# Low halves of weight pieces: which come by an accumulating DMA, which by subtraction, and how far ahead they are split

## The chip, the core and the metric

The kernel runs on one NeuronCore of a Trainium2 chip. The metric is the device time of one execution, in microseconds (us). The core has a TensorE (PE in the profile; PEld is its weight load), a VectorE (DVE), a ScalarE (ACT), a GpSimd (POOL), and a SyncE (SP) that issues DMAs. Each engine works through its own instructions in order and waits for others by semaphores. DMAs run beside them on 16 DMA engines.

## The reference

Two blocks of two layers each, batch 1, 512 tokens, width 1024, all in float32. Cut to its structure:

```
for l in range(2):                          # first block
    proj = rms_norm(h, g_mix) @ w_in        # q, k, v, recurrence and gate
    h += concat(diff_attention, rg_lru * gelu) @ w_out
    h += square(relu(rms_norm(h, g_mlp) @ w_mlp_in)) @ w_mlp_out
    h += sigmoid(rms_norm(h, g_ple) @ w_ple_gate) * (p @ w_ple_proj)     # "PLE"
x = rms_norm(h, g_final)
for l in range(2):                          # second block
    proj = rms_norm(x, g_pre_mix) @ w_in_2  # pool, q, k, v and an indexer
    x += rms_norm(concat(pool_mixer, topk_attention) @ w_out_2, g_post_mix)
    x += rms_norm(square(relu(rms_norm(x, g_pre_ffn) @ w_ff1_2)) @ w_ff2_2, g_post_ffn)
```

## The kernel before

**Pieces.** The weights are cut into pieces of 128 partitions x 1024 float32 (512 KB; the indexer's pieces have 512 or 656 columns), listed in `PLAN` (L102) in the order in which TensorE uses them. A piece has two k-blocks. It is split into two float32r halves: `wh`, the value rounded by ScalarE (L201), and `wl`, what is left. A product is three matmuls: high by high, high by low and low by high, so a piece of 512 columns is 24 matmuls, eight times a group of three.

**How a piece gets there.** `w_load` (L181) loads it by SP's queue into one of two `raw` buffers. `w_conv` (L188) makes `wh` on ScalarE and then `wl` in one of two ways. For the weights named in `ON_POOL` (L103: `w_in`, `index`, `w_in_2`, `w_out`, `w_out_2`) and the first four pieces of `w_ff1_2`, ScalarE writes the negated high half into `wl` (L206) and GpSimd issues a DMA that adds the weights from HBM onto it (L209). For all others VectorE subtracts (L211). The very first piece is always subtracted on VectorE.

**How far ahead.** `take` (L223) hands a piece to the matmuls and calls `w_ahead` (L214) first. That loads and splits pieces up to `LC` (L32) positions further on in `PLAN`, up to `LH` for kept ones, and loads one more (`LD` less `LC`). `wh` and `wl` have three buffers each (L159), one more than `LC`: a new piece needs the buffers of the piece that ended last.

**Kept pieces.** `gemm_h` (L254) goes through its pieces twice, for two halves of the tokens. Some of them are put in `keep` and get buffers of their own (tag `F`, in a pool that is opened after the attention's pool `mx` has closed). `keep_in` (L295) is called when a stage opens (L383 to L385, L576); the indexer's kept pieces of the second layer are listed at L1439. A piece that was split before its name came into `keep` sits in the ordinary buffers.

**Order.** A planner with a cost model puts the instructions of each engine in order, by the order in which the program writes them and by priorities; `urgent` raises one, and `behind` (L111) pins one instruction behind another on its engine. `bcast` (L412) broadcasts a row of scales through TensorE; splits are pinned behind the last one. `rsqrt` (L380) runs on GpSimd and notes itself in `st["rsqrt"]`.

**Sums of squares.** `Stat.add` (L389) squares on ScalarE and adds to `acc` on the engine named by `eng`; `Stat.mean` (L398) sums over partitions with small matmuls (B<-ones,acc), after which `rsqrt` gives the norm's scale. In PLE (`ev_g`, L986) the sums `st4` and, in the second layer, `st5` are added on GpSimd.

The stages in order of time: first block layer 0 (to 652 us), layer 1 (to 1264), indexer and attention of the second block layer 0 (1264 to 1485), its feed-forward (to 1879), then the same for layer 1. In the second block the feed-forward begins with `w_out_2` and `w_ff1_2` by `gemm_h` (L393, L571).

Of the kernel before, what the change touches and what calls it, by code (L numbers as in the profile page):

```python
# [8 lines left out]
F32 = mybir.dt.float32  # L9
F32R = mybir.dt.float32r  # L10
I32 = mybir.dt.int32
# [14 lines left out]
PC = 1024  # L26
ORDER = {"w_out": (4, 5, 6, 7, 0, 1, 2, 3), "w_out_2": (2, 3, 0, 1, 4, 5, 6, 7)}
NX = 11

URGENT = 250  # L30

LD, LC, LH = 3, 2, 3  # L32
IDX_SCALE = 8 ** -0.5
ALL = slice(0, 512)
HALVES = (slice(0, 256), slice(256, 512))
# [66 lines left out]
PLAN = _plan()  # L102
ON_POOL = ("w_in", "index", "w_in_2", "w_out", "w_out_2")  # L103
# [3 lines left out]
def two_blocks_kernel(ctx: ExitStack, tc: tile.TileContext, io):  # L107
    nc = tc.nc
    V, A, G, SY = nc.vector, nc.scalar, nc.gpsimd, nc.sync

    def behind(r, last):  # L111

        tc.add_manual_dep(r.ins, last.name, mybir.DependencyInfo(
            mybir.DependencyClass.NoSync, mybir.DependencyReason.DATA), reason="issue order")
# [24 lines left out]
    xp = ctx.enter_context(tc.tile_pool(name="acts", bufs=1))  # L139
# [8 lines left out]
    class Tags:  # L148
# [5 lines left out]
        def __call__(self, tag, dt=None, shape=None):  # L154
# [1 line left out]
            return self.pool.tile(shape or sh, dt or d, name=nm(tag), tag=tag, bufs=n)  # L156

    C512 = [128, 512]
    P = Tags(xp, X=([128, 2, 512], F32R, NX), raw=([128, PC], F32, 2), wh=([128, PC], F32R, 3),  # L159
             wl=([128, PC], F32R, 3), sn=([128, 8], F32, 4), v4=([128, 4], F32, 4), ri=([128, 4], I32, 2),  # L160
             rh=([128, 4], F32, 2), rt=([128, 4], F32, 2), rs=([128, 4], F32, 3), acc=(C512, F32, 2),
             mn=([128, 1], F32, 6), sm=([128, 4], F32, 6), sq=([128, 8], F32, 3), iw=([128, 8], F32, 4),
             m8=([128, 8], F32, 6))
# [6 lines left out]
    st = {"i": 0, "ld": 0, "cv": 0}  # L170
    raws, his, los, keep = {}, {}, {}, {}
# [9 lines left out]
    def w_load():  # L181
        i = st["ld"]
        st["ld"] += 1
        n = PLAN[i][4] * PLAN[i][5]
        raws[i] = P("raw")
        SY.dma_start(raws[i][:, :n], where[i])

    def w_conv():  # L188
        i = st["cv"]
        st["cv"] += 1  # L190
        n = PLAN[i][4] * PLAN[i][5]
        r = raws.pop(i)
        h_, l_ = keep[PLAN[i]]() if PLAN[i] in keep else (P("wh"), P("wl"))
        if i == 0:
            for a in range(0, n, n // 2):
                b = slice(a, a + n // 2)
                A.activation(h_[:, b], r[:, b], AF.Copy)  # L197
                V.tensor_sub(l_[:, b], r[:, b], h_[:, b].bitcast(F32))
            his[i], los[i] = h_, l_
            return  # L200
        g = A.activation(h_[:, :n], r[:, :n], AF.Copy)  # L201
        if "bcast" in st:
            behind(g, st["bcast"].ins)
        if PLAN[i][0] in ON_POOL or PLAN[i][0] == "w_ff1_2" and PLAN[i][2] == 0:

            g = A.activation(l_[:, :n], r[:, :n], AF.Copy, scale=-1.0)  # L206
            if "bcast" in st:
                behind(g, st["bcast"].ins)
            G.dma_start(l_[:, :n], where[i], accum_op=OP.add)  # L209
        else:  # L210
            V.tensor_sub(l_[:, :n], r[:, :n], h_[:, :n].bitcast(F32))  # L211
        his[i], los[i] = h_, l_
# [131 lines left out]
    h = [const.tile([128, S], F32, name=f"h{k}") for k in range(8)]  # L344
# [77 lines left out]
    X = [None] * 8  # L422
# [498 lines left out]
    def block1(l, X, fac, last):  # L921
        C = mix1(l, X, fac)
        X2, X3, X4 = [None] * 8, [None] * 8, [None] * 8
        with tc.tile_pool(name=nm("pp"), bufs=1) as ppool:
# [7 lines left out]
            with tc.tile_pool(name=nm("ff"), bufs=1) as fp:  # L932
# [10 lines left out]
                for g in range(2):  # L943
                    run(gemm_t(C[0:4], "w_out", l, g * 512, 4, 4, [bank() for _ in range(4)],
                               lambda c, p_, g=g: ev_o(g * 4 + c, p_)))
# [20 lines left out]
            with tc.tile_pool(name=nm("pl"), bufs=1) as lp:  # L966
                L = Tags(lp, prj=(C512, F32, 8), t=(C512, F32, 3),
                         q=(C512, F32, 2), sb=(C512, F32, 1))
                s3b = L("sb")

                s3 = P("v4")

                @urgent
                def mk_s3():
                    rsqrt(s3, st3.mean())

                st4, st5 = Stat(lambda: L("q")), Stat(lambda: L("q")) if last else None
                for g in range(2):
                    prj = []

                    def ev_p(c, p_):
                        t_ = L("prj")
                        A.activation(t_, p_, AF.Copy, scale=0.5)
                        prj.append(t_)

                    def ev_g(c, p_, g=g):  # L986
                        k = g * 4 + c
                        t_ = L("t")
                        V.tensor_mul(t_, p_, s3b)
                        A.activation(t_, t_, AF.Tanh, scale=0.5)  # L990
                        V.scalar_tensor_tensor(t_, t_, 1.0, prj[c], op0=OP.add, op1=OP.mult)
                        V.tensor_add(h[k], h[k], t_)
                        X4[k] = P("X")
                        split(X4[k], h[k], gff[:, k:k + 1] if last else col("g_mix", l + 1, k))
                        st4.add(h[k], eng=G)
                        if last:
                            st5.add(h[k], scale=col("g_final", 0, k), eng=G)

                    run(gemm_t(Pt, "w_ple_proj", l, g * 512, 0, 2, [bank() for _ in range(4)], ev_p))
                    run(gemm_t(X3, "w_ple_gate", l, g * 512, 0, 8, [bank() for _ in range(4)], ev_g),  # L1000
                        at={1: mk_s3, 4: lambda: bcast(s3, s3b)} if g == 0 else None)
# [25 lines left out]
    for l in range(DEPTH):  # L1027
        X, fac = block1(l, X, fac, l == DEPTH - 1)
# [468 lines left out]
    for l in range(DEPTH):  # L1497
        X, fac, ahead = block2(l, X, fac, ahead, l == DEPTH - 1)
# [74 lines left out]
```

## Time and profile before

| | us |
|---|---|
| median of 3 runs (2511.75 to 2515.87) | 2513.86 |
| the profiled execution's own time | 2513.39 |
| its span, first to last instruction | 2511.6 |
| TensorE busy | 2395.1 (95%) |
| VectorE busy | 1290.8 (51%) |
| ScalarE busy | 1197.6 (48%) |
| GpSimd busy | 297.2 (12%) |

The time outside the span is 1.8 us. "Busy" counts instructions that run; a waiting engine is idle, and the profile names what ended the wait. A line's number is that of the kernel before; most instructions of VectorE and TensorE go through a helper at L126, so they are told apart by their tiles.

### The profile page before, as it was taken

The numbers are of one execution on the slowest core, as the hardware profiler recorded it, in microseconds if no ns is written. First come the engines' busy times: TensorE is split into PE (matmuls) and PEld (weight loads), VectorE is DVE, ScalarE is ACT, GpSimd is POOL, SyncE is SP. The second block draws the span as 40 slices with busy tenths as digits, with TensorE's granted clock in tenths as the row PEclk, the third lists the DMA queues.
The fourth block names the chain that finished last, engine by engine and source line by source line (L and its number), as shares of the span: only waits on it lengthen the run. The fifth ranks groups of instructions, "written<-read, shape, count | busy, mean of one in ns | idle before, by whom it ended". The sixth has DMA issues, their size and how long they took to land.

```text
span 2511.6 us, 30853 instructions
## 1 busy us (share of the span) xinstructions
PE 2395.1 (95%) x11700; PEld 1993.6 (79%) x11700; DVE 1290.8 (51%) x2524; ACT 1197.6 (48%) x2051; POOL 297.2 (12%) x509
## 2 busy tenths in 40 slices
PE   7999999999999999999989989999998998999997
PEld 5778888888777888888778778888897777888887
DVE  4586433435458643343549847323345974632434
ACT  5785322324578532242456875323336587432321
POOL 1310000000231000000143212000012311100000
PEclk8999999999999999999989999999999999999999
DMA  7744233332774432333267452323345736232232
GB/s 191 166 103 125 93 94 99 93 96 89 167 168 101 111 99 93 101 93 94 79 144 157 113 129 73 101 93 93 101 107 125 168 83 136 68 101 92 93 101 68
DMA packets 80647, 276.19 MB, mean 110 GB/s; under 512 B 9073, under 2 KB 11505, under 8 KB 80497
## 3 DMA queue, kind: packets, MB, share of 16 engines
q1 hardware_dynamic: 62208, 211.22, 27.0%
q0 software_dynamic: 18288, 62.99, 14.6%
q8 instruction: 92, 1.51, 0.2%
q14 instruction: 59, 0.48, 0.1%
HBM read 272.08 MB, written 2.10 MB: 109 GB/s over the span
## 4 chain that ended last, share of the span: by engine, by line
PE 77%; DVE 9%; ACT 8%; DMA 3%; issue 2%; POOL 1%; SPq 0%; DVEq 0%; POOLq 0%; ACTq 0%
PE B L126 77%; ACT xe L643 1%; DVE ac L126 1%; DMA wl<-in_w 1%; DMA F<-in_w 1%; DVE fo L126 1%; DVE m L126 1%; DVE xe L126 1%; ACT wh L201 1%; DVE rn L126 1%; DVE X L126 1%; POOL acc L396 1%; DVE h L126 1%; ACT xe L1259 1%; ACT wl L206 1%
## 5 line engine op out<-in xcount | busy, mean ns | idle before, releaser
L126 PE MATMUL B<-X,wh 128*128 128x512 f32 (+1 forms) x3072 | 952.4, 392 | 7.0 <-ACT wh L197 7.0
L201 ACT ACTIVATE wh<-raw 128x1024 fp32r<-128x1024 f32 (+2 forms) x370 | 386.5, 1046 | 837.3 <-PE B L126 810.8
L126 DVE TENSOR_TENSOR wl<-raw,wh 128x1024 fp32r<-128x1024 f32 (+1 forms) x262 | 321.8, 1229 | 740.3 <-ACT wh L201 738.9
L126 PEld LDWEIGHTS B<-X,wh 128*128 128x128 f32 x3072 | 561.7, 189 | 111.5 <-ACT wh L197 7.0
L126 PE MATMUL B<-X,wl 128*128 128x512 f32 (+1 forms) x1536 | 596.3, 388 | 17.5 <-DMA wl<-in_w 16.0
L126 PE MATMUL B<-F,wh 128*128 128x512 f32 (+1 forms) x2048 | 608.6, 381 | 0.0
L126 PEld LDWEIGHTS B<-F,wh 128*128 128x128 f32 x2048 | 375.8, 188 | 81.9
L126 PE MATMUL B<-F,wl 128*128 128x512 f32 (+1 forms) x1024 | 389.9, 381 | 0.0
L126 PEld LDWEIGHTS B<-X,wl 128*128 128x128 f32 x1536 | 290.4, 189 | 78.9 <-DMA wl<-in_w 16.9
L126 PE MATMUL B<-wh,X 128*128 128x512 f32 (+2 forms) x960 | 293.7, 382 | 1.3 <-DMA wh<-in_wx 0.8
L126 PEld LDWEIGHTS B<-F,wl 128*128 128x128 f32 x1024 | 192.3, 188 | 40.9
L126 PEld LDWEIGHTS B<-wh,X 128*128 128x128 f32 x960 | 177.5, 192 | 33.2 <-issue 1.9
L126 PE MATMUL B<-wl,X 128*128 128x512 f32 (+2 forms) x504 | 181.6, 375 | 11.3 <-DMA wl<-in_wx 7.1
L206 ACT ACTIVATE wl<-raw 128x1024 fp32r<-128x1024 f32 (+2 forms) x110 | 111.8, 1016 | 62.6 <-PE B L126 62.4
L209 POOL DMA_DIRECT2D wl<-in_w x99 | 87.0, 882 | 441.7 <-ACT wl L206 344.5
L126 DVE TENSOR_TENSOR f<-r 128x512 f32<-128x512 f32 (+1 forms) x136 | 89.8, 664 | 61.3 <-ACT r L562 61.2
L562 ACT ACTIVATE r<-B 128x512 f32<-128x512 f32 (+1 forms) x136 | 76.4, 566 | 86.4 <-PE B L126 83.6
L126 PEld LDWEIGHTS B<-wl,X 128*128 128x128 f32 x504 | 95.2, 196 | 28.2 <-DMA wl<-in_wx 7.6
L126 PE MATMUL B<-X,F 128*128 128x256 f32 x576 | 80.4, 298 | 26.3 <-DMA F<-in_w 15.9
L126 PEld LDWEIGHTS B<-X,F 128*128 128x128 f32 x576 | 75.2, 201 | 30.1 <-DMA F<-in_w 16.3
L381 POOL TENSOR_TENSOR v<-v,nhalf 128x4 f32<-128x4 f32 (+1 forms) x8 | 8.6, 1070 | 764.1 <-DVE v L126 764.1
L126 DVE TENSOR_TENSOR F<-f,F 128x512 fp32r<-128x512 f32 (+1 forms) x136 | 88.5, 654 | 1.3 <-ACT F L370 1.0
(214 smaller groups left out, 2495.3 us busy)
## 6 DMA issues: line engine op xcount, KB each, us to landing
raw<-in_w SPq DMA_DIRECT2D x380, 512.0 KB, 3.5
wl<-in_w POOLq DMA_DIRECT2D x99, 512.0 KB, 7.9
F<-in_w POOLq DMA_DIRECT2D x12, 512.0 KB, 8.3
raw<-in_wx SPq DMA_DIRECT2D x8, 328.0 KB, 3.2
h<-in_xT SPq DMA_DIRECT2D x8, 256.0 KB, 7.1
raw<-in_wx SPq DMA_DIRECT2D x8, 256.0 KB, 2.7
out<-h SPq DMA_DIRECT2D x16, 128.0 KB, 1.8
wl<-in_wx POOLq DMA_DIRECT2D x5, 328.0 KB, 5.3
```

The lines of the kernel that those rows point to most:

```text
L126: r = f(*a, **k)
L201: g = A.activation(h_[:, :n], r[:, :n], AF.Copy)
L206: g = A.activation(l_[:, :n], r[:, :n], AF.Copy, scale=-1.0)
L209: G.dma_start(l_[:, :n], where[i], accum_op=OP.add)
L381: st["rsqrt"] = G.tensor_tensor(y, v, nhalf[:, :y.shape[-1]], op=OP.pow)
L396: eng.tensor_add(self.acc[:, ts], self.acc[:, ts], q_[:, ts])
L562: A.activation(r_[:, :n], p_, AF.Relu)
L643: A.activation(e[:, :n], e[:, :n], AF.Exp, scale=-1.0, bias=mn, accum_out=sums)
L1259: A.activation(e[:, :n], e[:, :n], AF.Copy, scale=sm[:, 1:2])
```

## The change

It raises `LD`, `LC` and `LH` from 3, 2, 3 to 4, 3, 4 and gives `wh` and `wl` a fourth buffer. The reserve for DMA descriptors is set to 8192 bytes per partition, half of what it is when not named. In `w_conv` the accumulating DMA stays for pieces of `ON_POOL` that are not the indexer's, not kept, and not among the first four of the plan. The other pieces that had it are subtracted: on VectorE those of the indexer's first layer, on GpSimd the rest (pieces 1 to 3 of `w_in`, the indexer's second layer, the kept ones), in two halves of the columns, pinned behind the last `rsqrt` that the program has written by then. The sum `st4` in PLE goes to VectorE.

By the code, of 127 accumulating DMAs 98 are left: 3 first pieces, 16 of the indexer, 2 of `w_out_2` and 8 of `w_ff1_2` no longer have one. Of the two kept pieces of `w_out_2` per layer the earlier one is now split before `keep_in` is called, so it sits in the ordinary buffers and keeps its DMA.

```diff
@@ -29,7 +29,7 @@
 
 URGENT = 250
 
-LD, LC, LH = 3, 2, 3
+LD, LC, LH = 4, 3, 4
 IDX_SCALE = 8 ** -0.5
 ALL = slice(0, 512)
 HALVES = (slice(0, 256), slice(256, 512))
@@ -156,8 +156,8 @@
             return self.pool.tile(shape or sh, dt or d, name=nm(tag), tag=tag, bufs=n)
 
     C512 = [128, 512]
-    P = Tags(xp, X=([128, 2, 512], F32R, NX), raw=([128, PC], F32, 2), wh=([128, PC], F32R, 3),
-             wl=([128, PC], F32R, 3), sn=([128, 8], F32, 4), v4=([128, 4], F32, 4), ri=([128, 4], I32, 2),
+    P = Tags(xp, X=([128, 2, 512], F32R, NX), raw=([128, PC], F32, 2), wh=([128, PC], F32R, 4),
+             wl=([128, PC], F32R, 4), sn=([128, 8], F32, 4), v4=([128, 4], F32, 4), ri=([128, 4], I32, 2),
              rh=([128, 4], F32, 2), rt=([128, 4], F32, 2), rs=([128, 4], F32, 3), acc=(C512, F32, 2),
              mn=([128, 1], F32, 6), sm=([128, 4], F32, 6), sq=([128, 8], F32, 3), iw=([128, 8], F32, 4),
              m8=([128, 8], F32, 6))
@@ -201,12 +201,18 @@
         g = A.activation(h_[:, :n], r[:, :n], AF.Copy)
         if "bcast" in st:
             behind(g, st["bcast"].ins)
-        if PLAN[i][0] in ON_POOL or PLAN[i][0] == "w_ff1_2" and PLAN[i][2] == 0:
+        if PLAN[i][0] in ON_POOL and PLAN[i][0] != "index" and PLAN[i] not in keep and i > 3:
 
             g = A.activation(l_[:, :n], r[:, :n], AF.Copy, scale=-1.0)
             if "bcast" in st:
                 behind(g, st["bcast"].ins)
             G.dma_start(l_[:, :n], where[i], accum_op=OP.add)
+        elif PLAN[i][0] in ON_POOL and PLAN[i][:2] != ("index", 0) or PLAN[i][0] == "w_ff1_2" and PLAN[i][2] == 0:
+            for a in range(0, n, n // 2):
+                b = slice(a, a + n // 2)
+                g = G.tensor_sub(l_[:, b], r[:, b], h_[:, b].bitcast(F32))
+                if "rsqrt" in st:
+                    behind(g, st["rsqrt"].ins)
         else:
             V.tensor_sub(l_[:, :n], r[:, :n], h_[:, :n].bitcast(F32))
         his[i], los[i] = h_, l_
@@ -992,7 +998,7 @@
                         V.tensor_add(h[k], h[k], t_)
                         X4[k] = P("X")
                         split(X4[k], h[k], gff[:, k:k + 1] if last else col("g_mix", l + 1, k))
-                        st4.add(h[k], eng=G)
+                        st4.add(h[k])
                         if last:
                             st5.add(h[k], scale=col("g_final", 0, k), eng=G)
 
@@ -1560,7 +1566,7 @@
     from concourse.bass_utils import run_bass_kernel_spmd as _run
 
     arrays = layout(inputs)
-    nc = _bacc.Bacc("TRN2", target_bir_lowering=False, num_devices=1)
+    nc = _bacc.Bacc("TRN2", target_bir_lowering=False, num_devices=1, dynamic_dma_scratch_size=8192)
     io = {}
     for name, a in arrays.items():
         io[name] = nc.dram_tensor(f"in_{name}", a.shape, mybir.dt.from_np(a.dtype), kind="ExternalInput").ap()
```

## Rows read from the trace of the kernel before

**Rows 1.** The page: span, busy times, landing times of DMAs (last number, us)
```profile
span 2511.6 us, 30853 instructions
...
PE 2395.1 (95%) x11700; PEld 1993.6 (79%) x11700; DVE 1290.8 (51%) x2524; ACT 1197.6 (48%) x2051; POOL 297.2 (12%) x509
...
raw<-in_w SPq DMA_DIRECT2D x380, 512.0 KB, 3.5
wl<-in_w POOLq DMA_DIRECT2D x99, 512.0 KB, 7.9
```

**Rows 2.** What TensorE waited for: us in total, times, longest
```profile
PE B L126 <- DMA wl<-in_w: 20.2, 3, 11.3
PE B L126 <- DMA F<-in_w: 15.9, 2, 8.0
...
PE B L126 <- DMA wl<-in_wx: 7.1, 2, 5.6
...
PE B L126 <- DMA F<-in_wx: 4.2, 2, 3.4
```

**Rows 3.** TensorE's timeline at its waits: start us, length, [idle before <- releaser]
```profile
26.61 0.80 PE L126 MATMUL B<-X,wl 128*128 128x512 f32 x1 [11.34 <-DMA wl<-in_w]
...
661.77 0.80 PE L126 MATMUL B<-X,wl 128*128 128x512 f32 x1 [4.67 <-DMA wl<-in_w]
...
1282.04 0.64 PE L126 MATMUL B<-wl,X 128*128 128x328 f32 x1 [5.56 <-DMA wl<-in_wx]
...
1308.01 0.50 PE L126 MATMUL B<-wl,X 128*128 128x512 f32 x1 [4.15 <-DMA wl<-in_w]
...
1493.34 7.01 PE L126 MATMUL B<-X,F 128*128 128x256 f32 x46 [7.87 <-DMA F<-in_w]
...
1896.49 3.37 PE L126 MATMUL B<-F,X 128*128 128x328 f32 x11 [3.40 <-DMA F<-in_wx]
...
2108.95 7.99 PE L126 MATMUL B<-X,F 128*128 128x256 f32 x46 [8.01 <-DMA F<-in_w]
```

**Rows 4.** Stretch after the first wait: length, busy us (count), PEclk, DMA share, GB/s
```profile
26.60:31.90 5.30, 5.29 (x12) 4.14 (x13) 0.00 (x0) 0.00 (x0) 0.00 (x0) 0.50 1.05 242
```

**Rows 5.** TensorE's timeline later in that piece, two neighbouring groups of three
```profile
33.52 0.62 PE L126 MATMUL B<-X,wh 128*128 128x512 f32 x2
...
34.20 0.62 PE L126 MATMUL B<-X,wh 128*128 128x512 f32 x2
```

**Rows 6.** GpSimd's timeline: the trigger behind the first wait, and one of the attention
```profile
17.55 1.04 POOL L209 DMA_DIRECT2D wl<-in_w  x1 [15.72 <-ACT wl L206]
...
1471.28 0.87 POOL L209 DMA_DIRECT2D wl<-in_w  x1 [4.60 <-ACT wl L206]
```

**Rows 7.** Groups of instructions: busy us, mean ns of one
```profile
L396 POOL TENSOR_TENSOR acc<-acc,q 128x256 f32<-128x256 f32 x42 | 35.9, 855 | 43.7 <-ACT q L395 42.3
L396 POOL TENSOR_TENSOR acc<-acc,q 128x512 f32<-128x512 f32 x21 | 33.7, 1621 | 50.8 <-ACT q L395 29.9 <-PE B L126 20.6
...
L126 DVE TENSOR_TENSOR wl<-raw,wh 128x1024 fp32r<-128x1024 f32 (+1 forms) x262 | 321.8, 1229 | 740.3 <-ACT wh L201 738.9 <-ACT wh L197 1.2
```

**Rows 8.** Before the indexer: GpSimd's last sums, TensorE's sums over partitions
```profile
1279.38 2.52 POOL L396 TENSOR_TENSOR acc<-acc,q 128x512 f32<-128x512 f32 x2 [1.09 <-ACT q L395]
...
1291.17 1.84 PE L126 MATMUL B<-ones,acc 128*128 128x1 f32 x16
```

**Rows 9.** ScalarE at the first kept piece after the attention
```profile
1482.30 1.06 ACT L201 ACTIVATE F<-raw 128x1024 fp32r<-128x1024 f32 x1 [0.81 <-DVE X L126]
```

**Rows 10.** VectorE beside GpSimd's sums, and VectorE alone, around 1880 us
```profile
1877.09 2.86 POOL L396 TENSOR_TENSOR acc<-acc,q 128x256 f32<-128x256 f32 x3 [0.88 <-ACT q L395]
...
1877.48 0.97 DVE L126 SCALAR_TENSOR_TENSOR X<-h,par,X 128x256 fp32r<-128x256 f32 x1
...
1884.29 0.47 DVE L126 SCALAR_TENSOR_TENSOR X<-h,par,X 128x256 fp32r<-128x256 f32 x1
```

**Rows 11.** The chain that ended last, in the first attention: start us, us
```profile
176.41 0.95 ACT wh L201
```

## The prediction

> **What bounds the kernel now.** I read the page first: TensorE is busy for 2395.1 of 2511.6 us [rows 1]. No faster matmul is in this change, so it can only win what TensorE waits, 116 us, and what it runs slowly after a wait. The list of TensorE's waits comes next. Its four largest entries by DMA are all low halves that an accumulating DMA had to finish: 20.2 + 15.9 + 7.1 + 4.2 = 47.4 us [rows 2]. TensorE's own timeline then says where they lie: at the start (11.34), at the first block's second layer (4.67), at the indexer's first layer (5.56) and the first `w_in_2` piece behind it (4.15), at each `w_out_2` (7.87 and 8.01), at the indexer's second layer (3.40) [rows 3]. These seven make 45.0; the rest, 2.4, are small ones beside them.
>
> A long wait costs more than itself. After the first one the granted clock of the stretch is 0.50, the lower level of 1.2 GHz, and 12 matmuls take 5.30 us [rows 4]. Later in the piece a group of three starts every 34.20 - 33.52 = 0.68 us [rows 5], 0.227 for one, so 12 would take 2.72: 2.6 us lost. The matmuls of 256 columns behind the two `w_out_2` waits take 7.01 and 7.99 us for 46 [rows 3]; an estimate at half of 0.227 each is 5.2, so 1.8 and 2.8 are lost. I put the seven at 2.2 on average, 15 us. What the change can win is thus about 47 + 15 = 62 us, and the question is what comes late next.
>
> **Part by part.** A DMA's landing takes 7.9 us at the median, the plain load 3.5 [rows 1]; a subtraction on VectorE takes 1.23 [rows 7]. GpSimd's sum of 512 columns, two inputs like a subtraction, takes 1.62 and of 256 columns 0.86 [rows 7], so I take 1.62 for a half of a piece, 3.2 for a piece, and about 1.0 for a half of an indexer's piece. That GpSimd writes float32r here shows in no row; the bounds are the two rows, 1.23 and 3.2 for a piece, and I take the latter, the same engine. A piece of 512 columns lasts eight groups, 5.44 us.
>
> *Start.* TensorE stops at 26.61 - 11.34 = 15.27. The trigger stood at 17.55 [rows 6] and landed 9.06 later. By subtraction the first half is there at 17.55 - 1.05 (the negation, gone) + 1.62 = 18.1 at the latest, and before 15.27 if GpSimd starts right behind the high half. Then piece 4 is late: it keeps its DMA and is needed at 15.3 + 3 x 5.44 = 31.6. With two `raw` buffers its load waits for piece 2's subtraction, which I put at 20.5 (one high half and one subtraction behind piece 1's): 20.5 + 3.5 + two passes of 1.05 + 0.9 + 7.9 = 34.9, so 3.3 late, and 1.6 for the clock. Won: 11.34 + 2.6 - 4.9 = 9.0, between 5 (also 2.9 late at piece 1, and its clock) and 13.9.
>
> *Second layer of the first block.* The pieces keep the DMA but are split one piece, 5.44, earlier, more than the wait of 4.67. Won 4.67 + 2, less a little: 6.5, between 4 (the load itself late) and 6.7. The cover is the third piece in hand; without it the wait stays.
>
> *PLE, indexer, first `w_in_2` piece.* Here lie 5.56 + 1.5 + 4.15, and 4.2 of slow clock by the average: 15.4. VectorE gets 8 subtractions of about 0.7 and, in each PLE, 8 sums of about 0.65, half of 1.23; GpSimd is rid of 8 sums of 1.62 in each, 13 us. TensorE comes to the sums over partitions at 1291.17 and doesn't wait; GpSimd's last two sums ended at 1279.38 + 2.52 = 1281.9 [rows 8]. With the waits ahead of it gone (5.56 + 1.5 + 2.5) TensorE is there at 1281.6, just when the sums end: 0 to 3 us, I take 1.5. The `w_in_2` piece keeps its DMA. It is split one indexer piece (3.5) earlier, but ScalarE's work before it hangs on the same scales: of its 4.15 I leave 2. Won 15.4 - 3.5 = 12, between 6 (3 + 4.15 and their clock) and 17 (no wait, and sooner splits in PLE).
>
> *The two `w_out_2` and `w_ff1_2`.* The earlier of the two kept pieces goes into the ordinary buffers with its DMA. The split that uses the same freed buffers was triggered at 1471.28 [rows 6], so it lands at 1479.2, and is needed at 1493.34 - 7.87 = 1485.47. The later one can't start before the attention's pool closes: its high half ran at 1482.30 [rows 9]; now it ends at 1483.4, and GpSimd's halves follow at 1485.0 and 1486.6. It is needed at 1485.47 + 2.7 = 1488.2. So the wait goes: 7.87 + 1.8 in layer 0, 8.01 + 2.8 in layer 1. What is late next is the norm. GpSimd now has 4 pieces of `w_ff1_2`, 13 us in eight halves, and queued behind them are the `rsqrt` of `mean_o`, which TensorE's broadcast waits for, and the sums `st2`; one half ahead costs 1.62, a piece 3.2. VectorE, which makes the next X there, takes 0.97 instead of 0.47 beside GpSimd [rows 10]. I take 2.6 off each: won 7 and 8, between 2.5 and 9.7, and 3.5 and 10.8.
>
> *The indexer's second layer.* 3.40 + 1.6 beside it + 2.6 of clock = 7.6. GpSimd gets 16 halves of about 1.0 for 8 triggers of 0.9: 9 us more, in the stage where VectorE makes X for both token halves. I take off 3.6: won 4, between 0 and 7.6.
>
> *The rest at nothing.* Three ahead with four buffers still lets a piece be split when the piece before the current one has ended, so ScalarE's place to wait is the same; cover is the planner's order (a rival below). The smaller descriptor reserve: triggers took 0.87 and 1.04 us [rows 6], no row shows one waiting for room. If room were short, a trigger would wait for a landing, 7.9 us at most; with a trigger every 5.44 and landings of 7.9 two are under way, so I take none.
>
> Sum: 9.0 + 6.5 + 12 + 7 + 8 + 4 = 46.5 us, between 21 and 65.7. The profiled execution took 2513.4, 1.8 more than its span, so 2466.9; the median is 0.5 above it: **2467 us**.
>
> **Rivals.**
>
> *The next wait takes more.* Two `raw` buffers remain, so a load still waits for the subtraction two pieces back, and GpSimd's subtraction holds the buffer for 3.2 where the negation held it for 1.05. For it speaks the start's piece 4; against it, that 29 DMAs less leave the DMA engines freer where their share was 1.05 [rows 4]. With all lower ends: 2514 - 21 = 2493.
>
> *GpSimd blocks VectorE.* Beside GpSimd's sums an instruction of VectorE took 0.50 longer [rows 10]. If one instruction of VectorE stood still for a whole half, the stages where VectorE feeds TensorE would pay 20 x 1.62 + 16 x 1.0 = 48 us, of which 8.8 are counted: 2506. The Trainium skill, SBUF — State Buffer, section "Who interferes with whom", states that a VectorE instruction with two SBUF inputs and a GpSimd instruction that reads SBUF exclude each other for the whole instruction. By that rule, 2506; the trace agrees that there is interference, but with 0.50, not with a full block each time.
>
> *Slower: splits ahead of the softmax.* Splits lie on ScalarE between the attention's exponentials; one is on the chain that ended last, with 0.95 us [rows 11]. Eight pieces are woven into each of the four attentions, 32 in all. If the planner, looking one piece further, puts both passes of each ahead of an exponential that TensorE waits for, that is 32 x 1.9 = 61: 2467 + 61 = 2528. It turns the sign from 25 pieces on (46.5 / 1.9). Against it: the same number of passes stands there now, and few of them are on the chain.
>
> *It doesn't remove the lateness.* If the load, not the accumulation, ended last at these places, the waits keep their length under another name: 2513. Against it: at the start the negation had run and the trigger stood at 17.55, so the load had landed by then [rows 6].
>
> *More than forecast.* All upper ends: 2448.
>
> **How the numbers follow.** The forecast (2455 to 2480) gets 0.55, the later next wait 0.20, the blocked VectorE 0.08, the splits ahead of the softmax 0.07, no effect 0.03, the full gain 0.07. The range 2448 to 2500 takes in the first, the second and the last, and leaves out 0.18. About 0.2%, 5 us, is what a measurement of this kernel can tell from no change. Faster by more: 0.55 + 0.20 + 0.07 and 0.06 of the blocked VectorE, 0.88; same 0.05; slower 0.07.
>
> **What would show it.** In the profile after, TensorE's waits for DMA into `F`, `wl` of the indexer and the first `wl` are gone; a wait for a DMA remains at about 31 us and near the first `w_in_2` piece. GpSimd's busy time changes little (26 halves of 1.62 and 16 of 1.0 come, 58 us; 29 triggers of 0.9 and 16 sums of 1.62 go, 52), VectorE's rises by some 16 us. Waits of TensorE for GpSimd's `rs`, or for VectorE's X around the norms, that are several us longer would show the second or third case; exponentials that wait behind splits the slow one. The forecast is wrong if TensorE's waits fall by less than 21 us in sum.

## The result, and the profile after

The changed kernel takes 2472.7 us in the median of 4 runs (2470.62 to 2473.18), the kernel before beside it 2514.86 (2511.75 to 2516.59, 4 runs): the ratio is 0.9832, 95% interval 0.9815 to 0.9849, 42 us faster. The forecast was 2467, 2448 to 2500.

From the page of the changed kernel, the lines that answer to [rows 1]:

```profile
span 2471.3 us, 30898 instructions
...
PE 2385.2 (97%) x11700; PEld 1983.4 (80%) x11700; DVE 1318.8 (53%) x2546; ACT 1176.7 (48%) x2022; POOL 299.1 (12%) x508
...
wl<-in_w POOLq DMA_DIRECT2D x98, 512.0 KB, 7.7
```

The span is 40.3 us shorter. TensorE issues the same 11700 matmuls; its idle time falls from 116.5 to 86.1, 30.4 us, its busy time by 9.9, while its mean granted clock rises from 0.984 to 0.994. An accumulating DMA still takes 7.7 us to land: the change made fewer of them matter, none of them faster.

What TensorE waited for in the changed kernel (answers to [rows 2]):

```profile
PE B L126 <- DVE X L126: 10.6, 12, 2.7
PE B L126 <- DVE acc L126: 8.0, 4, 2.8
...
PE B L126 <- DMA wl<-in_w: 4.9, 2, 3.5
...
PE B L126 <- DVE wl L126: 2.3, 1, 2.3
```

The 47.4 us of waits for DMAs are 4.9; the waits for DMAs into `F` and into the indexer's `wl` are gone (the `wl` in the last line is an indexer's piece that VectorE now subtracts). VectorE came in their place: 10.6 us for X (5.2 before), 8.0 for `acc` (2.8). Where that is shows TensorE's timeline after (answers to [rows 3]):

```profile
35.05 0.50 PE L126 MATMUL B<-wl,X 128*128 128x512 f32 x1 [1.40 <-DMA wl<-in_w]
...
1259.31 0.42 PE L126 MATMUL B<-wl,X 128*128 128x328 f32 x1 [2.32 <-DVE wl L126]
...
1281.92 0.77 PE L126 MATMUL B<-wl,X 128*128 128x512 f32 x1 [3.50 <-DMA wl<-in_w]
...
1471.78 0.61 PE L126 MATMUL B<-ones,acc 128*128 128x1 f32 x4 [2.60 <-DVE acc L126]
...
2078.02 0.61 PE L126 MATMUL B<-ones,acc 128*128 128x1 f32 x4 [2.44 <-DVE acc L126]
```

Behind each `w_out_2`, where 7.87 and 8.01 us stood, the sums over partitions of the norm now wait for `acc`.

To place the gain I cut each trace at the same eight instructions of TensorE, those that start at the given time in the kernel before. Lengths of the stages in us, of one profiled execution of each kernel:

| stage of the kernel before | before | change | lead alone | subtractions, old lead | one line alone | VectorE, 3 `raw` | forecast gain | gain |
|---|---|---|---|---|---|---|---|---|
| start to 84.05 | 84.05 | 76.63 | 82.82 | 73.41 | 84.00 | 74.77 | 9.0 | 7.4 |
| to 707.25: second layer | 623.20 | 615.83 | 616.15 | 615.64 | 616.07 | 615.60 | 6.5 | 7.4 |
| to 820.79 | 113.54 | 113.25 | 113.84 | 113.32 | 114.64 | 113.32 | 0 | 0.3 |
| to 1392.71: PLE, indexer, `w_in_2` | 571.92 | 560.90 | 560.74 | 562.74 | 570.44 | 565.22 | 12 | 11.0 |
| to 1535.00: first `w_out_2` | 142.29 | 138.61 | 140.19 | 138.05 | 142.09 | 135.16 | 7 | 3.7 |
| to 2006.81: indexer, layer two | 471.81 | 467.87 | 466.68 | 466.44 | 471.53 | 466.49 | 4 | 3.9 |
| to 2151.63: second `w_out_2` | 144.82 | 138.18 | 141.57 | 139.92 | 142.49 | 136.50 | 8 | 6.6 |
| to 2498.45 | 346.82 | 346.86 | 347.05 | 347.22 | 346.82 | 346.83 | 0 | 0.0 |

The last two columns compare the prediction with the change; the others are experiments below. Of the 6.6 at the second `w_out_2`, 1.4 lies in the attention before it and is a matter of the clock (last section); at the place itself it is 5.2.

What happened at 1471.78 us is on three engines' timelines of the changed kernel. ScalarE:

```profile
1463.35 1.06 ACT L201 ACTIVATE F<-raw 128x1024 fp32r<-128x1024 f32 x1 [2.63 <-DMA raw<-in_w]
1466.55 1.06 ACT L201 ACTIVATE F<-raw 128x1024 fp32r<-128x1024 f32 x1 [2.14 <-DMA raw<-in_w]
1467.52 0.71 ACT L401 ACTIVATE q<-fo 128x256 f32<-128x256 f32 x2
```

GpSimd:

```profile
1457.34 5.50 POOL L213 TENSOR_TENSOR F<-raw,F 128x512 fp32r<-128x512 f32 x4 [10.98 <-ACT F L201]
1464.49 2.55 POOL L213 TENSOR_TENSOR F<-raw,F 128x512 fp32r<-128x512 f32 x2 [1.65 <-ACT F L201]
1467.69 2.70 POOL L213 TENSOR_TENSOR F<-raw,F 128x512 fp32r<-128x512 f32 x2 [0.65 <-ACT F L201]
1472.14 2.52 POOL L213 TENSOR_TENSOR F<-raw,F 128x512 fp32r<-128x512 f32 x2 [1.75 <-ACT F L201]
1474.62 0.72 POOL L387 TENSOR_TENSOR rs<-v,nhalf 128x2 f32<-128x2 f32 x1
```

VectorE:

```profile
1459.85 3.28 DVE L126 TENSOR_TENSOR acc<-acc,q 128x256 f32<-128x256 f32 x3
...
1464.18 1.46 DVE L126 TENSOR_TENSOR fo<-B,X 128x256 f32<-128x256 f32 x4 [1.06 <-PE B L126]
...
1467.95 3.77 DVE L126 TENSOR_TENSOR acc<-acc,q 128x256 f32<-128x256 f32 x4 [2.30 <-ACT q L401]
```

The operands `fo` are there by 1465.6, but the squares `q` start only at 1467.52: in front of them in ScalarE's queue stands a split that waits for its load. The load waits for a `raw` buffer, which GpSimd's subtraction holds for 2.7 us more. Then the four sums take 3.77 us, but not 0.94 each: a row of the timeline can merge several instructions, and one by one GpSimd's two halves and VectorE's first three sums are

```profile
1467.69 1.29 POOL L213 TENSOR_TENSOR F<-raw,F 128x512 fp32r<-128x512 f32 x1 [0.65 <-ACT F L201]
1468.94 1.44 POOL L213 TENSOR_TENSOR F<-raw,F 128x512 fp32r<-128x512 f32 x1
```

```profile
1467.95 1.31 DVE L126 TENSOR_TENSOR acc<-acc,q 128x256 f32<-128x256 f32 x1 [2.30 <-ACT q L401]
1469.36 1.30 DVE L126 TENSOR_TENSOR acc<-acc,q 128x256 f32<-128x256 f32 x1
1470.77 0.42 DVE L126 TENSOR_TENSOR acc<-acc,q 128x256 f32<-128x256 f32 x1
```

Each of the first two ends 0.28 us after the half that was running when it began; the third, with GpSimd idle, takes 0.42, as all four do in the kernel before from 1501.06. So a sum that meets a subtraction stands until that is over, 0.9 us here, and the two together lose 1.8. That the squares start 1.9 us after their operands is the other part. So two causes are in line, and the experiments ask which counts.

### The profile page after: what moved, and what is told of

The parts are those of the page before. It is cut to its first block, busy times and chain, and to the rows that moved or that the text cites. A ratio compares the mean times of both kernels' runs of the same rounds, so it can differ in the third digit from the quotient of the medians.

```text
span 2471.3 us, 30898 instructions
## 1 busy us (share of the span) xinstructions
PE 2385.2 (97%) x11700; PEld 1983.4 (80%) x11700; DVE 1318.8 (53%) x2546; ACT 1176.7 (48%) x2022; POOL 299.1 (12%) x508
## 4 chain that ended last, share of the span: by engine, by line
PE 74%; DVE 12%; ACT 8%; issue 3%; DMA 1%; POOL 1%; SPq 0%; DVEq 0%; ACTq 0%; POOLq 0%
PE B L126 74%; DVE ac L126 2%; DVE m L126 2%; ACT xe L649 1%; DVE fo L126 1%; DVE X L126 1%; DVE xe L126 1%; DVE rn L126 1%; ACT wh L201 1%; DMA raw<-in_w 1%; ACT wl L206 1%; DVE h L126 1%; DVE acc L126 1%; POOL F L213 1%; ACT xe L1265 1%
## 5 line engine op out<-in xcount | busy, mean ns | idle before, releaser
L126 DVE TENSOR_TENSOR wl<-raw,wh 128x1024 fp32r<-128x1024 f32 (+1 forms) x270 | 326.8, 1211 | 741.9 <-ACT wh L201 740.7
L126 PEld LDWEIGHTS B<-X,wh 128*128 128x128 f32 x3136 | 570.6, 189 | 110.6 <-ACT wh L197 6.9
L126 PE MATMUL B<-X,wl 128*128 128x512 f32 (+1 forms) x1568 | 603.4, 385 | 0.0
L126 PEld LDWEIGHTS B<-X,wl 128*128 128x128 f32 x1568 | 296.0, 189 | 59.7 <-DVE wl L126 0.2
L206 ACT ACTIVATE wl<-raw 128x1024 fp32r<-128x1024 f32 x98 | 103.2, 1054 | 46.3 <-PE B L126 43.0
L126 PE MATMUL B<-ks,qs 128*128 128x256 f32 (+2 forms) x352 | 83.9, 333 | 4.5 <-DVE qs L126 2.0
L376 ACT ACTIVATE F<-f 128x512 fp32r<-128x512 f32 (+1 forms) x136 | 81.6, 603 | 5.7 <-DVE f L126 3.5
```

The lines of the kernel that those rows point to most:

```text
L126: r = f(*a, **k)
L376: A.activation(dst[:, 0, :], src, AF.Copy)
```

## The experiments

Theory after the result: what is missing against the forecast is at the two `w_out_2`, and GpSimd's subtraction makes it, by stopping VectorE's sums (A) or by holding the `raw` buffer, so that ScalarE's split waits with the squares behind it (B). Rivals: the lead reorders ScalarE, or VectorE's new sums do it. The first four runs were on one chip, beside the kernel before at 2511.91 us.

**Only the lead.** The kernel before with:

```diff
-LD, LC, LH = 3, 2, 3
+LD, LC, LH = 4, 3, 4
-wh=([128, PC], F32R, 3), wl=([128, PC], F32R, 3)
+wh=([128, PC], F32R, 4), wl=([128, PC], F32R, 4)
-nc = _bacc.Bacc("TRN2", target_bir_lowering=False, num_devices=1)
+nc = _bacc.Bacc("TRN2", target_bir_lowering=False, num_devices=1, dynamic_dma_scratch_size=8192)
```

> Half of the change alone: splits one piece further ahead, with the fourth buffers of wh and wl and the smaller DMA scratch, while the first, index and kept pieces still get their low parts by accumulating DMAs and the PLE's sums stay on GpSimd. Theory (the lead hides a landing that is late by less than a piece, and does nothing at the start): the start stays at 84 us for its 820.79-family anchor chain, the DMA waits of 4 to 6 us at the index pieces mostly go, the two waits of 7.9 and 8.0 us on the kept pieces keep at least half: about 2495 us. Rival (lead alone is the whole of the change, the subtractions bring only the start's 7.4 us): about 2480 us. Rival (lead only moves ScalarE's work ahead of other ScalarE work): 2515 us or more.

2486.97 us, ratio 0.9901 (0.9887 to 0.9916). Of what the lead leaves, TensorE's timeline shows:

```profile
25.51 0.79 PE L126 MATMUL B<-X,wl 128*128 128x512 f32 x1 [8.88 <-DMA wl<-in_w]
...
1271.59 0.38 PE L126 MATMUL B<-wl,X 128*128 128x256 f32 x1 [3.93 <-DMA wl<-in_wx]
...
1473.64 4.40 PE L126 MATMUL B<-X,F 128*128 128x256 f32 x22 [4.39 <-DMA F<-in_w]
```

The time lies between my 2495 and the rival's 2480. By the table the lead alone does everything that the change does at the second layer, at PLE and indexer, and at the indexer's second layer (560.74 and 466.68 are no longer than the change's). It doesn't reach the start, and at `w_out_2` a wait of 4.39 stays.

**Only the subtractions.** The changed kernel with:

```diff
-LD, LC, LH = 4, 3, 4
+LD, LC, LH = 3, 2, 3
```

> The other half: first, kept and index pieces by subtraction and the PLE's sums on VectorE, but the splits as far ahead as before (two pieces, three for kept ones). Theory (the waits removed were landings of accumulating DMAs, and a subtraction removes them without lead): start 7.4 us, the second layer's index pieces 7 us, both places of the kept pieces 3 to 5 us each as in the changed kernel; what is missing is the first piece of w_in_2 in steady flow, which keeps an accumulating DMA and has one piece less of lead (3.5 us of wait in the changed kernel, 5 us more without the lead): about 2480 us. Rival (the lead is needed at each place, since the split itself waits for its load): 2495 us or more. Rival (the lead costs as much as it brings): 2470 us or less.

2472.15 us (2471.85 to 2472.58), ratio 0.9842 (0.9827 to 0.9857): the change's time without its lead, nearest to the last of the three cases. The wait that I expected to grow by 5 us, at the first `w_in_2` piece, is 3.79 instead of 3.50. The lead and the rest of the change are two cures of the same waits: 25 us by the one and 40 by the other, beside the same kernel before; with both it is 2472.7 us, so the lead adds nothing that these runs can tell (the 42 of the result is against another measurement of the kernel before, 2514.86). At the start the lead even costs 3.2 us, 76.63 against 73.41, and as much with the kept pieces on VectorE (77.96 against 74.72, runs below). One caution: the fourth buffers of `wh` and `wl` stayed in this run.

**The PLE's sums back on GpSimd.** The changed kernel with:

```diff
-st4.add(h[k])
+st4.add(h[k], eng=G)
```

> The changed kernel with the PLE's sums of squares back on GpSimd. Theory: the sums come late again at the PLE's end (two adds of 2.5 us on GpSimd in the kernel before), in front of the matmul with ones, and nothing is queued there on VectorE that would gain: 3 to 5 us slower, 2476 to 2478 us, all of it between the anchors at 1259 and 1282 us. Rival (the move is hidden, TensorE waits there for the low parts of the index piece and of w_in_2 anyway): within 0.5 us of 2472.7 us.

2473.04 us (2472.01 to 2475.66): the rival's time. Beside the rest of the change this line brings nothing.

**The same line alone.** The reverse, in the kernel before (2509.93 us beside it):

```diff
-st4.add(h[k], eng=G)
+st4.add(h[k])
```

> The kernel before with one line of the change alone: the PLE's sums of squares of the second norm on VectorE. Theory (TensorE's wait of 4.67 us at 661.8 us had two sufficient cures: splits further ahead, as the run with the PLE's sums back on GpSimd shows, and sums off GpSimd, where one trigger stood behind 3.4 us of them, as the runs with the old lead show): the wait at 661.8 us and its slow stretch go, 6 to 7 us; at the end of the second PLE, in front of the indexer, 0 to 3 us more; all other waits stay: 2502 to 2506 us. Rival (the wait went by the lead or by the spare buffers of wh and wl alone, as the prediction had it): the wait stays, within 2 us of the kernel before.

2501.91 us, ratio 0.9966 (0.9951 to 0.9980): 8 us from one line, 7.1 of them in the second layer, where the wait of 4.67 us at 661.77 [rows 3] is gone. GpSimd's timeline of the kernel before, just ahead of that wait, shows a part of why:

```profile
643.11 3.45 POOL L396 TENSOR_TENSOR acc<-acc,q 128x512 f32<-128x512 f32 x2
648.53 3.43 POOL L396 TENSOR_TENSOR acc<-acc,q 128x512 f32<-128x512 f32 x2 [1.98 <-ACT q L395]
...
652.52 1.79 POOL L209 DMA_DIRECT2D wl<-in_w  x2 [0.30 <-issue]
```

and ScalarE's:

```profile
644.67 1.06 ACT L201 ACTIVATE wh<-raw 128x1024 fp32r<-128x1024 f32 x1
...
649.62 1.05 ACT L206 ACTIVATE wl<-raw 128x1024 fp32r<-128x1024 f32 x1
```

The high half was ready at 645.7; its negation ran only at 649.62 and the trigger at 652.52, behind GpSimd's sums. Of this the sums delay the trigger by 1.9 us (the negation ended at 650.67). With the line moved, the negation of the same piece runs at 645.77 and the trigger at 647.11, 5.4 us sooner: ScalarE's order changed too, with the negation ahead of two X, and no run separates the two. So this wait had two sufficient cures, the lead and this line, and what the line is worth can only be seen without the lead.

**`w_ff1_2` by DMA.** The changed kernel with the kept pieces of `w_ff1_2` back on accumulating DMAs:

```diff
-if PLAN[i][0] in ON_POOL and PLAN[i][0] != "index" and PLAN[i] not in keep and i > 3:
+if (PLAN[i][0] in ON_POOL and PLAN[i][0] != "index" and PLAN[i] not in keep and i > 3
+        or PLAN[i][0] == "w_ff1_2" and PLAN[i][2] == 0):
```

> The changed kernel with the kept pieces of w_ff1_2 alone back on accumulating DMAs (w_out_2 still by subtraction). Theory (the subtractions on GpSimd slow VectorE's sums at these two places from 0.47 to 0.96 us and hold the rsqrt, which takes some 3 us of the gain at each place): VectorE's sums go back to about 0.5 us and the waits for acc of 2.6 and 2.4 us shrink below 1.5 us, but a wait for the DMA of F comes back with 3 to 8 us at each of the two places: 2476 to 2486 us. Rival (one piece more of lead has by itself hidden the landing of F): no wait on F, 2467 to 2470 us, faster than the change as it is. Rival (what is missing there is not from GpSimd, but from the split that waits for its load): the sums stay late by the same 2.5 us, and the time is that of the change plus the DMA's wait.

2482.71 us, ratio 0.9881 (0.9866 to 0.9896). Its VectorE, its TensorE and its ScalarE:

```profile
1469.85 2.01 DVE L126 TENSOR_TENSOR acc<-acc,q 128x256 f32<-128x256 f32 x4 [4.67 <-ACT q L402]
```

```profile
1471.91 0.61 PE L126 MATMUL B<-ones,acc 128*128 128x1 f32 x4 [3.21 <-DVE acc L126]
```

```profile
1463.52 1.06 ACT L201 ACTIVATE F<-raw 128x1024 fp32r<-128x1024 f32 x1 [3.27 <-DMA raw<-in_w]
1464.48 1.04 ACT L207 ACTIVATE F<-raw 128x1024 fp32r<-128x1024 f32 x1
1467.50 1.06 ACT L201 ACTIVATE F<-raw 128x1024 fp32r<-128x1024 f32 x1 [1.98 <-DMA raw<-in_w]
1468.47 1.04 ACT L207 ACTIVATE F<-raw 128x1024 fp32r<-128x1024 f32 x1
```

The sums are fast again, 0.42 each with 0.1 between them, and TensorE waits longer, 3.21 instead of 2.60 (and 4.66 instead of 2.44 at the second place); no wait for `F` came back. That is against A as the only cause and for B: the split waits for its load, and two passes per piece stand before the squares. The theory's time came true for another reason: the loss (3.3 us at the first place, 3.1 at the second) sits in splits that wait for loads with squares or X behind them in ScalarE's queue, not in the DMA of `F`. It also says that the subtraction of `w_ff1_2` on GpSimd, with its faults, is worth 9.7 us (against the 2473.04 of the same set); 1.4 of them lie in the second attention, where the clock can fall either way (last section).

The next four ran together, beside 2509.97 us.

**Kept pieces on VectorE.** The changed kernel with:

```diff
-elif PLAN[i][0] in ON_POOL and PLAN[i][:2] != ("index", 0) or PLAN[i][0] == "w_ff1_2" and PLAN[i][2] == 0:
+elif PLAN[i][0] in ("w_in", "index") and PLAN[i][:2] != ("index", 0):
```

so that the last branch takes them.

> The changed kernel with the kept pieces of w_out_2 and w_ff1_2 subtracted on VectorE, one instruction each, instead of two halves on GpSimd. Theory A (VectorE's sums beside GpSimd's subtractions, 0.96 against 0.47 us, and the rsqrt behind them make the 2.6 and 2.4 us waits for acc): the sums take 0.5 us, the rsqrt starts 0.3 us after its operand, the waits for acc go below 1 us at both places: 2466 to 2469 us. Theory B (the squares come late because they are queued on ScalarE behind a split that waits for its load; the load waits for the raw buffer that the subtraction holds): VectorE frees the buffer some 1.5 us sooner per piece, the splits' waits for the load shrink from 2.6 and 2.1 to about 1 us: 2467 to 2470 us. Rival (VectorE's own queue becomes the bound there: four pieces of 1.2 us stand before sums and evictions): 2474 us or more.

2470.41 us (2468.26 to 2473.59), ratio 0.9836. The splits wait 0.37 and 0.83 us for their loads, the sums take 0.42 each, the `acc` waits are 1.63 and 1.34. The two places win 2.6 and 1.1 us against the change. The direction is as expected, the size half; in the whole time its runs overlap with those of the change.

**A third `raw` buffer, GpSimd as in the change.** The room comes from the spare `wh` and `wl`:

```diff
-LD, LC, LH = 4, 3, 4
+LD, LC, LH = 4, 2, 3
-raw=([128, PC], F32, 2), wh=([128, PC], F32R, 4), wl=([128, PC], F32R, 4)
+raw=([128, PC], F32, 3), wh=([128, PC], F32R, 3), wl=([128, PC], F32R, 3)
```

> The changed kernel with the splits only as far ahead as in the kernel before (two and three) and the room of the two spare buffers of wh and wl given to a third raw buffer, so that loads run one piece further ahead; all subtractions as in the change. It is compared with the run that had the subtractions without the lead (2472.2 us). Theory B (a split that waits for its load, with the squares queued behind it): no split of a kept piece waits for its load, the squares start some 2 us sooner, the waits for acc of 2.5 and 2.2 us shrink to 1 us or less: 2468 to 2470 us. Theory A (the slow sums beside GpSimd are the cause): the sums still take 0.96 us and the waits for acc stay above 2 us: 2472 us. Rival (more loads in flight delay the accumulating DMAs at the start and at w_in_2): 2475 us or more.

2477.34 us (2476.55 to 2478.40), ratio 0.9866: slower than without, the rival's time. It should have told A from B and didn't, since the splits wait as before, 2.61 and 2.07 us. Its GpSimd:

```profile
1459.19 13.54 POOL L213 TENSOR_TENSOR F<-raw,F 128x512 fp32r<-128x512 f32 x10 [10.99 <-ACT F L201]
```

Five pieces in 13.54 us without a gap, 2.7 each: with three buffers as with two, GpSimd's pace sets when one comes free. Of the 5.2 us lost against the run with only the subtractions, 2.5 lie at the indexer.

**`w_in_2`, a miss.** The changed kernel with one piece of `w_in_2` of either layer on VectorE:

```diff
-if PLAN[i][0] in ON_POOL and PLAN[i][0] != "index" and PLAN[i] not in keep and i > 3:
+if PLAN[i][0] in ON_POOL and PLAN[i][0] != "index" and PLAN[i] not in keep and i > 3 and not (PLAN[i][0] == "w_in_2" and PLAN[i][2] == 0 and PLAN[i][3] == 0):
-elif PLAN[i][0] in ON_POOL and PLAN[i][:2] != ("index", 0) or PLAN[i][0] == "w_ff1_2" and PLAN[i][2] == 0:
+elif PLAN[i][0] != "w_in_2" and (PLAN[i][0] in ON_POOL and PLAN[i][:2] != ("index", 0) or PLAN[i][0] == "w_ff1_2" and PLAN[i][2] == 0):
```

> The changed kernel with the first piece of w_in_2 of either layer subtracted on VectorE in place of its accumulating DMA. Theory (the 3.5 us wait of TensorE at 1281.9 us is this DMA's landing, and the next piece's DMA, issued at 1277.2, lands before it is needed): the wait goes, the next piece waits under 1 us: 2469 to 2470 us. Rival (the next piece, whose DMA is issued 4.4 us later, takes its place): a DMA wait of 2 to 3.5 us one piece later, 2472 to 2473 us.

2473.45 us (2473.06 to 2474.80). The condition names the group with columns from 0, and the first one in `PLAN` has columns from 512; so it moved a piece that nothing waits for, and the wait stayed, at 3.10 us. It says nothing on the wait; in this set it stands for the change, from which it differs by one piece per layer.

**Third `raw` buffer and kept pieces on VectorE.** Both edits above.

> The third raw buffer and the kept pieces on VectorE together. If A and B each remove their own part, the two waits for acc are gone and the time is 2464 to 2467 us; if they remove the same 4 to 5 us, it is that of the better of the two runs within 1 us; if VectorE's queue binds, it is above the run with the third buffer alone.

2467.92 us (2466.62 to 2470.21), ratio 0.9830 (0.9815 to 0.9844), 5.5 below the stand-in for the change, with no run of the one within those of the other, and 0.9 above the first case's 2467. As in that case, TensorE's sums over partitions don't wait:

```profile
1471.32 0.54 PE L126 MATMUL B<-ones,acc 128*128 128x1 f32 x4
```

The stage is 135.16 us against 142.29 before: the gain there is 7.1, and at the second place 8.2 (122.56 to 114.37, counted from 2029.07), the forecast's 7 and 8. It loses 4.3 at the indexer, where TensorE waits 3.80 for VectorE's `wl` and 4.01 for the `w_in_2` piece.

The next three ran together, beside 2511.51 us.

**The fourth corner.** Kept pieces on VectorE, two `raw` buffers, old lead.

> Kept pieces on VectorE, with the splits as far ahead as in the kernel before and two raw buffers: the fourth corner beside the runs with GpSimd and two (2472.2 us), GpSimd and three (2477.3 us), and VectorE and three raw buffers (2467.9 us). Theory (GpSimd's 2.7 us per piece is what holds the buffers, so that VectorE alone removes the cause): 2467 to 2469 us. Rival (the third buffer is needed beside VectorE): 2471 to 2473 us.

2470.18 us (2467.54 to 2473.36), between the two cases. The two stages with `w_out_2`, counted from 1413.62 and 2029.07, last 117.1 and 117.6 with GpSimd and two buffers, 118.7 and 120.1 with GpSimd and three, 115.7 and 117.2 with VectorE and two, 114.2 and 114.4 with VectorE and three. The third buffer pays only once GpSimd is out of the way.

**The indexer's first layer on GpSimd.** The run with both edits, and:

```diff
-elif PLAN[i][0] in ("w_in", "index") and PLAN[i][:2] != ("index", 0):
+elif PLAN[i][0] in ("w_in", "index"):
```

> The run with the third raw buffer and the kept pieces on VectorE (2467.9 us), with the first layer's index pieces subtracted on GpSimd in halves instead of on VectorE. Theory (TensorE's wait of 3.8 us at 1256 us is VectorE's in-order queue, where the index piece's subtraction stands behind the PLE's sums; GpSimd is idle there until 1250, and the stretch at half clock that follows the wait goes with it): the wait shrinks below 1 us and the granted clock of 1257 to 1260 us is 1.0: 2463 to 2465 us. Rival (GpSimd's own sums, 1.3 to 2.3 us each, and the two engines slowing one another make up for it): 2467 to 2469 us.

2468.38 us (2467.99 to 2469.35), the rival's. The wait of 3.80 became 1.65 (now for GpSimd), the clock of 1256 to 1260 us rose from 0.62 to 1.00, and the `w_in_2` piece behind it waits 5.87 instead of 4.01: the time only moved on to the next landing, 1.0 us net.

**And the first two `w_in_2` pieces on GpSimd.** This time the right group:

```diff
-if PLAN[i][0] in ON_POOL and PLAN[i][0] != "index" and PLAN[i] not in keep and i > 3:
+if PLAN[i][0] in ON_POOL and PLAN[i][0] != "index" and PLAN[i] not in keep and i > 3 and not (PLAN[i][0] == "w_in_2" and PLAN[i][2] == 512 and PLAN[i][3] < 4):
-elif PLAN[i][0] in ("w_in", "index"):
+elif PLAN[i][0] in ("w_in", "index", "w_in_2"):
```

> The run before it in this call, with the first two pieces of w_in_2 of its first group (columns from 512, of which the first is the one that TensorE waits for at 1282 to 1284 us) subtracted on GpSimd in place of their accumulating DMAs. The earlier run on w_in_2 had moved a piece of the group with columns from 0, which is not the first in order, and left this wait as it was. Theory (the wait of 3.5 to 4 us is the landing of that DMA, and GpSimd subtracts both pieces within 6 us while TensorE has index work): no wait above 1 us there and a higher granted clock after it: 3 to 5 us below the run before it. Rival (the third piece takes the wait over, or GpSimd's index scaling is held up and the indexer with it): within 1 us of the run before it.

2466.23 us (2463.29 to 2468.56), ratio 0.9824 (0.9802 to 0.9846), 2.2 below the run before it, between the theory's 3 to 5 and the rival's 1; the runs of the two overlap. The 5.87 us wait is gone, the stage is 3.7 shorter (560.50); a new wait of 3.12 for VectorE's `qs` stands behind it, and in the second layer one of 3.59 for `ix` takes 2.4 back. It is the fastest kernel here; it did not run beside the change, and the intervals of their ratios overlap.

## Why the prediction was right, point by point

**What bounds it** held: the waits for accumulating DMAs and the slow stretches behind them are what moved, 30.4 us of idle and 9.9 of busy time.

**Start**, 9.0 forecast, 7.4 measured. GpSimd's halves took 1.27 to 1.80 against the 1.62, and piece 4 was late by 1.40 instead of 3.3; but a wait of 1.90 for the broadcast `sb` at 39.07, which I had not looked for, came behind. It is the lead's: ScalarE's copy for `sb` stands behind a split that waited 4.22 us for its load (at 36.53), and with the old lead TensorE doesn't wait for it and the start gains 10.6.

**Second layer**, 6.5 and 7.4: right in size, and the lead that I named does suffice. But I wrote that the wait stays without the third piece in hand, and that is wrong: it went with the old lead too, and with one line, `st4`, alone. I had priced `st4` only by who waits for the sums, not by the trigger that is queued behind them on GpSimd.

**PLE, indexer, `w_in_2`**, 12 and 11.0. The remaining wait for the `w_in_2` piece was put at 2 and is 3.50; the 1.5 for the sums is nothing beside the change. Lead alone wins 11.2 here, so the indexer's subtractions in the first layer bring nothing in its presence.

**The two `w_out_2`**, 7 and 8 forecast, 3.7 and 5.2 measured: the mis-sized term. The waits for `F` went, as worked out, and 2.6 us for the norm was the right size for what is late next (2.60 and 2.44). What failed is the slow stretch, 1.8 and 2.8, which I counted as won, and the waits for X, which the 2.6 was to cover too. At the first place TensorE's waits between the two anchors fall from 16.7 to 12.4, 4.3, but the rest of the stage grows by 0.6 instead of shrinking by 1.8; 0.9 more goes to X (2.25 before, 3.13 after). At the second, from 2029.07 on, the waits fall by 3.4 and the rest by 1.8 of the 2.8, and 1.7 more goes to X (2.18 and 3.90). At the first place a wait of 2.6 brings a slow stretch of its own. The windows of the kernel before and of the changed one (columns as in [rows 4], with the engines' busy times between):

```profile
1492.00:1496.00 4.00, 2.66 (x12) 2.66 (x13) 0.00 (x0) 1.12 (x2) 0.00 (x0) 0.50 1.06 261
```

```profile
1472.00:1476.00 4.00, 4.00 (x25) 4.00 (x25) 2.33 (x7) 1.69 (x5) 3.20 (x3) 0.64 0.42 132
```

Before, 2.66 us at 0.50 lose 1.3; after, 4.00 at 0.64 lose 1.4. With the `acc` wait away, as in the run with VectorE and three buffers, the window reads:

```profile
1473.00:1477.00 4.00, 4.00 (x36) 4.00 (x35) 3.79 (x12) 3.54 (x7) 0.00 (x0) 1.00 0.04 12
```

and the whole forecast gain is there. The path to the norm's lateness was another than I wrote, too: not the `rsqrt` behind GpSimd's halves first of all (it started 2.0 us after its operand, at 1474.62, but TensorE waits for it 0.33 at the second place and not at the first), but the squares behind a split and the sums that stand still.

**Indexer's second layer**, 4 and 3.9. The lead alone wins 5.1, the subtractions with the old lead 5.4.

**Rivals.** "The next wait takes more" had the mechanism, a subtraction that holds the `raw` buffer, and it showed at `w_out_2`; its price was some 6 us (3.3 and 2.8 under the forecast there), not 25. "GpSimd blocks VectorE" had its mechanism right, and my case against it was misread: the 0.50 of [rows 10] is not a slowing, but what was left of the sum that GpSimd was in. One by one, in the kernel before:

```profile
1877.09 1.08 POOL L396 TENSOR_TENSOR acc<-acc,q 128x256 f32<-128x256 f32 x1 [0.88 <-ACT q L395]
```

VectorE's X of 1877.48 ends at 1878.45, 0.28 after it. In the changed kernel eight sums of 256 columns began when a subtraction of 512 columns had 1.0 us still to run; all eight ended 0.28 to 0.29 after it and took 1.30 to 1.33 instead of 0.42, while `fo<-B,X`, with one of its two inputs in PSUM, took its 0.42 beside GpSimd all the same. The Trainium skill's rule (SBUF — State Buffer, "Who interferes with whom"), exclusion for the whole instruction where VectorE has two inputs in SBUF, agrees with that. What failed in the rival is its price: not each of the 42 subtractions meets such an instruction. By an estimate, which counts the length above the shortest of the same kind, VectorE stood behind them for 17 us in all, not 48, and not all of that reached TensorE, whose waits for VectorE's X and `acc` rose by 10.6 us, B's share included. "Splits ahead of the softmax" and "doesn't remove the lateness" didn't come.

**Signs.** GpSimd's busy time rose by 1.9 us (6 forecast), VectorE's by 28 instead of 16, TensorE's waits fell by 30.4, above the 21 that I had named. A VectorE that stands behind GpSimd counts as busy: by the same estimate, over all of GpSimd's work, that is 47 us after and 34 before, 13 more, about the 12 that I missed. The waits for a DMA that I expected to remain are there, at 35.05 and 1281.92.

What stays open: how much of the `acc` wait A alone makes, since the run meant to remove B didn't. From the rows at 1471.78 an estimate is that the 1.8 of A and the 1.9 of B lie in line for a wait of 2.6, so that either cure alone leaves some 0.7 to 0.8. Open is also whether the lead without any spare buffer would do what it did.

## What to carry to other kernels

A late arrival can have several sufficient cures (further ahead, another engine, a shorter queue): try each alone before adding them, since 25 us and 40 us apart (8 of them by one line) made no more than the 40 together. A move to an idle engine is priced by how long it holds the buffers that the next load needs, by what stands behind it in the queues, and by what it stops on another engine, not by its busy share. Where a wait shrinks but doesn't vanish, don't count the slow stretch behind it as won in full. A merged row gives a mean; a mean of 0.94 hid two sums of 1.3 and two of 0.42, so look at single instructions before you call an engine slowed.

## What the runs showed of the hardware

The same wait can be followed by either level of TensorE's clock. The wait of 2.32 us for the indexer's `wl` is followed, in the changed kernel and then in the run with the old lead, by:

```profile
1259.30:1262.00 2.70, 2.69 (x18) 2.70 (x19) 1.91 (x4) 0.91 (x2) 0.00 (x0) 1.00 0.47 126
```

```profile
1257.00:1260.30 3.30, 3.30 (x14) 3.30 (x13) 2.21 (x5) 2.38 (x4) 0.62 (x1) 0.52 0.61 178
```

2.4 GHz in the one, 1.2 for nearly all of the stretch in the other; that is 1.6 of the 1.8 us by which the two differ in this stage. A wait of 2.25 in the second attention does the same, 22.26 us of stage in the kernel before and 20.84 in the changed one, with nothing of the change near it. What decides between them no row here shows; it is some 1.5 us that can fall either way with an edit elsewhere. And GpSimd's subtraction of 512 columns with a float32r result took 1.35 us (the 20 into `F`, mean 1352 ns), less than the sum of 512 columns that I priced it by (1.62), while VectorE does 1024 columns in 1.2. Both of GpSimd's means hold waits for VectorE: 14 of the 20 subtractions took 1.28 to 1.30, and the quickest seven of the 21 sums 1.26 to 1.30.
